# Gate maxima by scan instructions, a split last tile in the first output projection, one slab pool with two early weights, and low halves of the output weights on VectorE, in a two-layer hybrid decoder step

## The chip, the cores and the metric

The kernel runs on one NeuronCore of a Trainium2 chip. The metric is the device time of one execution in microseconds (us). The engines are TensorE (PE in the rows), VectorE (DVE), ScalarE (ACT) and GpSimd (POOL), each with an instruction queue of its own; all DMAs of this kernel are issued on the queue of SyncE (SP).

## The reference, cut to what matters

One step of a two-layer trunk for a prompt of 1024 positions and eight samples of one position each, 1032 columns in all, in float32, with 1024 features.

```python
h = x
# layer 0
u = rmsnorm(h) @ w_in_even            # q|k|v|gate | z|xBC|dt
att = dilated_attention(q, k, v) * silu(gate)
y   = rmsnorm(ssd_scan(conv(xBC), dt) * silu(z))
h   = h + concat(att, y) @ w_out_even # 1536 -> 1024
# layer 1
u = rmsnorm(h) @ w_in_odd             # q|k|v|o|i|f|z
bcum = cumsum(log_sigmoid(f))         # in chunks of 128
m_t  = maximum(bcum + m_prev, running max of (bcum_t - bcum_s + i_s))
m_new = max(b_last + m_prev, max(b_last - bcum + i))   # carried over 8 chunks
h = h + (mlstm(q, k, v, m_t) * silu(z)) @ w_out_odd    # 2048 -> 1024
y = rmsnorm(h)
```

## The kernel before, in words

Activations lie transposed, features on the partitions and columns along the free axis. Every large product is made of three matmuls in a rounded float32 type: each operand is split into a high half (a cast on ScalarE, L91) and a low half (a subtraction, L92, on VectorE or GpSimd), and high x high, high x low and low x high are summed in PSUM. Weights come by DMA as 128x1024 tiles into three raw buffers (L94) and are split by the class `Weights` (L116), whose list `engs` names the engines that take the low halves in turn; `next` keeps one weight ahead.

Slabs (`S`, L57) are [128,1040] tiles of a pool of 15; layer 0 and layer 1 each open such a pool of their own, layer 1 after layer 0 has closed (L1107, L1110). TMP (L78) is a pool of four [128,520] tiles that residuals, squares, gate values and loads share. `eap` (L575) has two [128,512] tiles.

The order in which the work is written down is not the order on the engines: a planner in the build puts instructions of each engine in an order by that writing order and by when it expects operands and buffers to be free. Small closures are put between matmul groups by hand: `bpump` takes from the list `bg`, `dpump` from `dq` (the samples' attention and the samples' state steps), `slot` from `gsteps` (the gates of layer 1).

The stages that the change touches, in order of time:

- Gates z of layer 0 (L990 to L1032): twelve weights f, three column chunks c each. After f < 8 and c == 2 one step of the samples' state (`dss_step`, L825) is taken from `dq`, two at f == 6; a step uses two TMP tiles (`dso`, L831) and GpSimd and VectorE in turn (L835 to L838). Chunks with f >= 8 also load the attention into TMP (`al`, L1006).
- First output projection (`wqo`, L987, all low halves on GpSimd; L1082 to L1102): two column halves hv (512 and 520 columns), eight output tiles f each, `out_f` (L914). In hv = 0 the second half's operand is made beside it by `mix_y(1)` (L867): eight gate products (L884) with `z` loaded into TMP (L874), squares and their sum (L213), then the column norm by matmuls with a vector of ones (`stat_r`, L184), a broadcast (`r_bcast`, L203), and the splits. In hv = 1 the norm of layer 1 for the first half is made (`xn1_piece(0)`, L1048).
- The boundary (L1103, L1104): after the last tile, `xn1_piece(1)` makes norm and operands `yh`, `yl` for the 520 columns of the second half; six of its eight low halves are on GpSimd (L1064). Layer 1 then opens its pools, its first two weights are split (L1504), and for each of three column chunks of 344 two projections run, with the gate projections `pg` (L1151) after chunks 0 and 1 and after chunk 2 (L1506 to L1511).
- Gates of layer 1 (L1183 to L1231): a running maximum over 128 positions in seven doubling steps of two VectorE instructions (L1191, L1192), and a recurrence over eight chunks on one partition, two instructions each (L1199, L1200).
- Second output projection (`wqf`, L1569, low halves on VectorE and GpSimd in turn; L1631 to L1670). Its last tile is already done in two column pieces: `out_f` with `done` (L940) finishes a piece, starts its norm, and puts these steps between the matmuls of the next piece (L946).

Of the kernel before, what the change touches and what calls it, by code (L numbers as in the profile page):

```python
# [21 lines left out]
SLABS0 = 15  # L22
SLABS1 = 15
# [6 lines left out]
def body(ctx, tc, I, O):  # L30
# [15 lines left out]
    dr = pool("dr", 1, space=DRAM)  # L46
    cur = {}

    def scope(tag, slabs):
        st = ctx.enter_context(ExitStack())  # L50
        cur["stack"] = st
        cur["cst"] = pool("cst" + tag, 1, st)
        cur["sm"] = pool("sm" + tag, 2, st)
        cur["slab"] = pool("slab" + tag, slabs, st)
        return st

    def S(name, dt=F32):  # L57
        return cur["slab"].tile([128, 1040], dt, tag="S", name=name)
# [97 lines left out]
    layer0 = scope("0", SLABS0)  # L156
# [565 lines left out]
    def ssd_prep(c, g):  # L722
# [7 lines left out]
        if c > 0:  # L730
            ea = eap.tile([128, 512], F32, tag="ea", name="ea")
# [135 lines left out]
    def mix_y(hv, alloc):  # L867
# [46 lines left out]
    def out_f(wq, nk, ops, hv, res, dst, done=None):  # L914
# [72 lines left out]
    wqo = Weights([(I["wo0"][j], 1024) for _ in range(2) for j in range(12)], (G,))  # L987
    gA = []
    ssd_pump(1)
    for f in range(12):  # L990
# [11 lines left out]
        for c in range(3):  # L1002
# [10 lines left out]
            if f < 8:  # L1013
# [3 lines left out]
                if c == 2:  # L1017
                    dpump(1 + (f == 6))
# [29 lines left out]
    def xn1_piece(hv, src):  # L1048
        n = 520 if hv else 512
        c0 = 512 * hv  # L1050
        box = {}

        def stat():
            box["r"] = stat_r([hacc[:, hv * 520 : hv * 520 + n]], n, 1.0 / 1024, 1.0)
# [4 lines left out]
        def out(k):  # L1059
            if hv == 0:  # L1060
# [3 lines left out]
            sink(src(k)[:, :n], normw[:, 1, k : k + 1], box["p"], hi, lo, G if hv and k % 4 < 3 else V, xsm[:, k] if hv else None)  # L1064

        bg.extend([stat, bcast])
        bg.extend(lambda k=k: out(k) for k in range(8))

    def h1_reload(k):
        t = eap.tile([128, 512], F32, tag="ea", name="h1r")  # L1070
# [7 lines left out]

    h1 = None
    ops = [[operand(hv, u) for u in range(2)] for hv in range(2)]  # L1080
    wst = wstream(wqo)
    for hv in range(2):  # L1082
# [4 lines left out]
        for f in range(8):  # L1087
            dst = pairs(h1)(f, 0, n) if hv else None
            dst = out_f(wst, 12, ops, hv, I["xT"][:, f, c0 : c0 + n], dst)
# [9 lines left out]
            elif f == 1:  # L1099
                xn1_piece(0, h1_reload)  # L1100
# [9 lines left out]
    layer1 = scope("1", SLABS1)  # L1110
    cur["w"] = pool("wp1", 2, layer1)
    wq1 = Weights([(I[n_][h, j], 1024) for h in range(8) for n_, cnt in (("wq", 4), ("wz", 2)) for j in range(cnt)], (V,))
# [27 lines left out]
    mp = C("mp", [1, 9, 8])  # L1140
# [3 lines left out]
    G.memset(mp[:, 0], -1e30)  # L1144
# [30 lines left out]
    def gates_b():  # L1175
        pb_ = X("pbc")
        PE.matmul(pb_[:, 0:64], tri, lff[:, 0:64], start=True, stop=True)
        PE.matmul(pb_[:, 64:128], ones, lff[:, 0:64], start=True, stop=True)
        V.tensor_copy(bcm, pb_[:, 0:64])
        V.tensor_copy(btot, pb_[:, 64:128])  # L1180
        V.tensor_tensor(av, igf[:, 0:64], bcm, sub)

    def gates_c2():  # L1183
# [4 lines left out]
        for j in range(7):  # L1188
            s_ = 1 << j
            a_, b_ = gp[j % 2], gp[(j + 1) % 2]  # L1190
            V.tensor_tensor(b_[:, s_:], a_[:, s_:], a_[:, : 128 - s_], mx)  # L1191
            V.tensor_copy(b_[:, :s_], a_[:, :s_])  # L1192

    def gates_d():
        gmax = gt["gp"][1]
# [5 lines left out]
        store(O["mm"], mp[:, 8])  # L1201

    def gates_e():
        gmax = gt["gp"][1]
        mpf = mp.rearrange("p a b -> p (a b)")
        pm = X("pmb")
        PE.matmul(pm[:, 0:72], ones[0:1, :], mpf, start=True, stop=True)
        PE.matmul(pm[:64, 128:129], mpf[:, 0:64], ones[0:1, 0:1], start=True, stop=True)
# [24 lines left out]
    gsteps = deque([gates_a, rest, rest, gates_b, rest, gates_c2, rest, gates_d, gates_e, rest, gates_f])  # L1233
# [335 lines left out]
    wqf = Weights([(I["wo1"][f][:, o * 1024 : o * 1024 + 1024], 1024) for _ in range(2) for f in range(8) for o in range(2)], (V, G))  # L1569
# [275 lines left out]
```

## Time and profile before

| | us |
|---|---|
| median of 3 runs | 2179.12 |
| lowest and highest run | 2178.77 and 2180.62 |
| the profiled execution's own time | 2182.44 |
| its span, first to last instruction | 2180.5 |
| idle time of TensorE within the span (2180.5 less 2104.4 busy) | 76.1 |

The profiled execution took 3.3 us more than the median. In the rows, PE is TensorE's matmul side and PEld its weight loads; a bracket at the end of a timeline row gives the engine's idle time before it and what ended that. PEclk is the granted share of TensorE's clock: 1.00 is 2.4 GHz and 0.50 is 1.2 GHz.

### The profile page before, as it was taken

How to read it: one execution, taken by the hardware profiler on the slowest of the kernel's cores; microseconds unless marked ns; L12 is line 12 of the kernel's file. 1: busy time of each engine (PE TensorE's matmuls, PEld its weight loads, DVE VectorE, ACT ScalarE, POOL GpSimd, SP SyncE). 2: the span in 40 equal slices, each digit the busy share in tenths (PEclk: the TensorE clock that was granted, in tenths of full speed). 3: DMA queues.
4: the chain of work that ended last, by engine and by line, in shares of the span. 5: the costliest groups of instructions: out<-in, count | busy, mean ns of one | idle time of the engine just before them, and what ended most of it. 6: DMA issues, size and time to landing. Idle time of an engine off the chain costs nothing.

```text
span 2180.5 us, 35187 instructions
## 1 busy us (share of the span) xinstructions
PE 2104.4 (97%) x12913; PEld 1884.0 (86%) x12913; DVE 1356.9 (62%) x3153; ACT 847.8 (39%) x1828; POOL 665.8 (31%) x1089
## 2 busy tenths in 40 slices
PE   7999988999899999999999999999999999999998
PEld 6877777998789798989989889898898998987798
DVE  7444388668887644844548566575565655756754
ACT  5434334455425332533425334253343433434331
POOL 4222143014552343052141321413214223242321
PEclk9999999999999999999999999999999999999999
DMA  4222152134555552311314123132241232406753
GB/s 158 71 74 77 41 158 76 53 99 157 170 188 158 163 187 66 107 45 40 95 38 133 57 89 125 33 115 79 81 131 29 95 100 67 150 24 208 251 172 100
DMA packets 161918, 232.29 MB, mean 107 GB/s; under 512 B 41170, under 2 KB 106690, under 8 KB 161746
## 3 DMA queue, kind: packets, MB, share of 16 engines
q1 hardware_dynamic: 161746, 230.04, 33.5%
q8 instruction: 102, 1.67, 0.3%
q14 instruction: 70, 0.57, 0.1%
HBM read 174.35 MB, written 55.62 MB: 105 GB/s over the span
## 4 chain that ended last, share of the span: by engine, by line
PE 56%; DVE 3%; POOL 2%; DMA 2%; issue 1%; ACT 1%; POOLq 0%; DVEq 0%; SPq 0%; ACTq 0%
PE pf L113 24%; PE pvo L113 16%; PE po L927 8%; PE mN L113 2%; PE mC L113 2%; PE mS L1275 1%; DMA dC<-in_mcs 1%; POOL mCl L92 1%; PE mH L1336 1%; PE mS L1277 1%; DVE dnum L1402 0%; DVE dC L1398 0%; DMA mE<-mud 0%; POOL md L1261 0%; PE prb L203 0%
## 5 line engine op out<-in xcount | busy, mean ns | idle before, releaser
L113 PE MATMUL pf<-yl,wh 128*128 128x344 f32 x1152 | 369.5, 321 | 2.1 <-POOL yl L92 2.1
L113 PE MATMUL pf<-yh,wh 128*128 128x344 f32 x1152 | 371.0, 322 | 0.0
L113 PE MATMUL pf<-yh,wl 128*128 128x344 f32 x1152 | 368.6, 320 | 0.2 <-DVE wl L92 0.2
L91 ACT CAST wh<-raw 128x1024 fp32r<-128x1024 f32 x128 | 133.8, 1046 | 228.8 <-PE pf L113 90.3
L113 PEld LDWEIGHTS pf<-yl,wh 128*128 128x128 f32 x1152 | 217.0, 188 | 3.0 <-POOL yl L92 3.0
L113 PEld LDWEIGHTS pf<-yh,wh 128*128 128x128 f32 x1152 | 216.8, 188 | 1.4 <-ACT craw L238 1.0
L113 PEld LDWEIGHTS pf<-yh,wl 128*128 128x128 f32 x1152 | 216.6, 188 | 0.8 <-DVE wl L92 0.7
L113 PE MATMUL pvo<-wvh,yh 128*128 128x512 f32 x512 | 205.8, 402 | 0.0
L113 PE MATMUL pvo<-wvl,yh 128*128 128x512 f32 x512 | 201.7, 394 | 0.0
L113 PE MATMUL pvo<-wvh,yl 128*128 128x512 f32 x512 | 201.6, 394 | 0.0
L113 PE MATMUL pf<-xh,wh 128*128 128x344 f32 x576 | 195.6, 340 | 2.7 <-ACT gth L232 2.7
L92 DVE TENSOR_TENSOR wl<-raw,wh 128x1024 fp32r<-128x1024 f32 x88 | 111.6, 1268 | 133.7 <-ACT wh L91 133.5
L113 PE MATMUL pf<-xh,wl 128*128 128x344 f32 x576 | 187.5, 326 | 0.0
L113 PE MATMUL pf<-xl,wh 128*128 128x344 f32 x576 | 187.5, 326 | 0.0
L92 POOL TENSOR_TENSOR wl<-raw,wh 128x1024 fp32r<-128x1024 f32 x40 | 99.3, 2483 | 220.0 <-ACT wh L91 220.0
L1263 DVE TENSOR_SCALAR mx<-mx,mbs,md 128x256 f32<-128x256 f32 x64 | 26.5, 413 | 177.3 <-POOL md L1262 177.3
L927 PE MATMUL po<-oh,wl 128*128 128x512 f32 (+2 forms) x384 | 123.9, 323 | 5.2 <-DVE wl L92 4.2
L246 DVE SCALAR_TENSOR_TENSOR cout<-craw,mcw,cout 128x1024 f32<-128x1024 f32 x96 | 123.1, 1283 | 8.3 <-ACT cout L244 6.8
L927 PE MATMUL po<-oh,wh 128*128 128x512 f32 (+2 forms) x384 | 124.1, 324 | 0.9 <-ACT oh L91 0.9
L927 PE MATMUL po<-ol,wh 128*128 128x512 f32 (+2 forms) x384 | 123.7, 322 | 0.0
L113 PEld LDWEIGHTS pf<-xh,wh 128*128 128x128 f32 x576 | 110.7, 192 | 8.8 <-issue 5.1
L113 PEld LDWEIGHTS pvo<-wvh,yl 128*128 128x128 f32 x512 | 96.1, 188 | 22.2
(435 smaller groups left out, 5200.4 us busy)
## 6 DMA issues: line engine op xcount, KB each, us to landing
raw<-in_wo SPq DMA_DIRECT2D x56, 512.0 KB
raw<-in_wq SPq DMA_DIRECT2D x32, 512.0 KB
raw<-in_wvo SPq DMA_DIRECT2D x32, 512.0 KB
dC<-in_mcs SPq DMA_DIRECT2D x32, 512.0 KB
out_mcs<-dC SPq DMA_DIRECT2D x32, 512.0 KB
raw<-in_wf SPq DMA_DIRECT2D x24, 512.0 KB
sE<-acd SPq DMA_DIRECT2D x16, 512.0 KB
raw<-in_wz SPq DMA_DIRECT2D x16, 512.0 KB
```

Source lines behind the costliest of these rows:

```text
L91: A.copy(hi, src)
L92: eng.tensor_tensor(lo, src, hi.bitcast(F32), sub)
L113: PE.matmul(out, l, r, start=i == 0, stop=i == n - 1)
L246: V.scalar_tensor_tensor(o[:, :NP], raw[:, j : j + NP], w4[:, j : j + 1], o[:, :NP], mult, add)
L927: PE.matmul(p[:, :m], wt[:, ws], at, start=i == 0 and q == 0, stop=i == nk - 1 and q == 2)
L1263: V.tensor_scalar(x, x, bs[:, 6:7], d[:, 2:3], sub, mult)
L1275: PE.matmul(pS[:, 0:128], hd["k"][j][:, tok], hd["q"][j][:, tok], start=j == 0, stop=j == 1)
L1277: PE.transpose(pS[:, 128 + j * 128 : 256 + j * 128], hd["k"][j][:, tok], ident)
L1336: PE.transpose(pH[:, j * 128 : j * 128 + 128], x[:, j * 128 : j * 128 + 128], ident)
```

## The change

Six edits. (1) The running maximum over 128 positions and the recurrence over eight chunks become one scan instruction each; the recurrence lies on eight partitions, one per head, and is brought there and back by small matmuls; one more `rest` is put into the list of gate steps. (2) The last tile of the first output projection goes through the two-piece path of `out_f`; each piece's norm follows it, with alternate low halves on GpSimd. (3) One pool of 15 slabs serves both layers. (4) The first two weights of layer 1 are fetched before and during that last tile, into slabs. (5) `z` of the second half loads into `eap` in place of TMP, and the samples' state steps come one position earlier (the last of them at f == 7, c == 0). (6) All low halves of both output projections' weights are on VectorE.

```diff
-    def scope(tag, slabs):
+    slab = pool("slab", SLABS)
+    def scope(tag):
...
-        def __init__(self, srcs, engs=(V,), first=()):
+        def __init__(self, srcs, engs=(V,), first=(), slabs=0):
...
-                th = p.tile([128, 1024], F32R, tag="wh", name="wh")
-                tl = p.tile([128, 1024], F32R, tag="wl", name="wl")
+                if self.slabs:
+                    self.slabs -= 1
+                    th, tl = (S(x, F32R)[:, :1024] for x in ("wh", "wl"))
+                else:
+                    th = p.tile([128, 1024], F32R, tag="wh", name="wh")
+                    tl = p.tile([128, 1024], F32R, tag="wl", name="wl")
...
-            z = TMP("zl") if hv else eap.tile([128, 512], F32, tag="ea", name="zl")
+            z = eap.tile([128, 520], F32, tag="ea", name="zl")
...
-                    if steps and i in (7, 11):
+                    if steps and i in ((7, 11) if nk == 16 else (4, 10)):
...
-    wqo = Weights([...], (G,))
+    wqo = Weights([...])
...
-                if c == 2:
-                    dpump(1 + (f == 6))
+                if c == 2 and f < 7 or f == 0 and c == 1 or f == 7 and c != 1:
+                    dpump(1)
...
-    def xn1_piece(hv, src):
+    def xn1_piece(c0, n, accs, src):
...
-            sink(src(k)[:, :n], normw[:, 1, k : k + 1], box["p"], hi, lo, G if hv and k % 4 < 3 else V, xsm[:, k] if hv else None)
-        bg.extend([stat, bcast])
-        bg.extend(lambda k=k: out(k) for k in range(8))
+            x = src(k)
+            scaled(x, x, normw[:, 1, k : k + 1], box["p"])
+            split(hi, lo, x, G if c0 and k % 2 else V)
+            if c0 == 512 and k == 7:
+                wq1.fetch()
+            if c0 + n == T:
+                split(xsm[:, k, 0:8], xsm[:, k, 8:16], x[:, n - 8 : n])
+        return [stat, bcast] + [lambda k=k: out(k) for k in range(8)]
+
+    def xn1_tail(dst, o, n):
+        store(h1d[7][:, 512 + o : 512 + o + n], dst[:, o : o + n])
+        sq = TMP("sq")[:, :n]
+        A.activation(sq, dst[:, o : o + n], AF.Square)
+        return xn1_piece(512 + o, n, [hacc[:, 520 + o : 520 + o + n], sq], lambda k: pairs(h1)(k, o, n))
...
+    wq1 = Weights([...], (V,), slabs=2)
...
+            if hv and f == 7:
+                bpump(40)
+                wq1.fetch()
+            dst = out_f(wst, 12, ops, hv, I["xT"][:, f, c0 : c0 + n], dst, xn1_tail if hv and f == 7 else None)
...
-    xn1_piece(1, lambda k: pairs(h1)(k, 0, 520))
-    bpump(40)
...
-        for j in range(7):
-            s_ = 1 << j
-            a_, b_ = gp[j % 2], gp[(j + 1) % 2]
-            V.tensor_tensor(b_[:, s_:], a_[:, s_:], a_[:, : 128 - s_], mx)
-            V.tensor_copy(b_[:, :s_], a_[:, :s_])
+        V.tensor_tensor_scan(gp[1], gp[0], gp[0], -1e30, mx, mx)
+        V.tensor_scalar(gr2[:, 0:8], blk[:64, 0:8], gp[1][:, 127:128], None, mult)
...
-        PE.transpose(pgl[:1, 0:64], gmax[:, 127:128], ident[:64, :64])
-        for c in range(8):
-            V.tensor_tensor(mp[:, c + 1], mp[:, c], pgl[:1, c * 8 : c * 8 + 8], mx)
-            V.tensor_tensor(mp[:, c + 1], mp[:, c + 1], btot[0:1, c * 8 : c * 8 + 8], add)
+        PE.matmul(pgl[:8, 0:16], selh, gr2, start=True, stop=True)
+        gl = SM("gl", [8, 16], 1)
+        V.tensor_copy(gl, pgl[:8, 0:16])
+        V.tensor_tensor_scan(mp[:, 1:9], gl[:, 0:8], gl[:, 8:16], -1e30, mx, add)
+        V.tensor_tensor(mp72, ident[:8, :8].unsqueeze(1).broadcast_to([8, 9, 8]), mp.unsqueeze(2).broadcast_to([8, 9, 8]), mult)
...
-    wqf = Weights([...], (V, G))
+    wqf = Weights([...])
```

## Rows read from the trace of the kernel before

**Rows 1.** The page, busy time of each engine in the whole span.

```profile
PE 2104.4 (97%) x12913; PEld 1884.0 (86%) x12913; DVE 1356.9 (62%) x3153; ACT 847.8 (39%) x1828; POOL 665.8 (31%) x1089
```

**Rows 2.** Busy time by stretch: boundary, gates of layer 1, rest of layer 1's heads.

```profile
core 0: us, PE busy (x) PEld busy (x) DVE busy (x) ACT busy (x) POOL busy (x), PEclk, DMA share, GB/s
...
837.60:883.02 45.42, 40.76 (x238) 36.16 (x238) 28.19 (x53) 18.46 (x37) 15.27 (x25) 0.92 0.11 28
883.02:927.54 44.52, 44.52 (x286) 43.52 (x286) 35.27 (x99) 21.01 (x39) 2.54 (x5) 1.00 0.45 122
927.54:1972.00 1044.46, 1037.90 (x6134) 945.26 (x6133) 625.81 (x1585) 399.90 (x827) 316.53 (x672) 1.00 0.26 81
```

**Rows 3.** The boundary: two timeline rows of PE, a wait, a chain row.

```profile
837.32 0.28 PE L927 MATMUL po<-ao,wl 128*128 128x256 f32 x1
839.62 1.18 PE L184 MATMUL pst<-ones,ssdst 128*128 128x1 f32 x10 [2.02 <-DVE ssdst L213]
...
PE pf L113 <- POOL yl L92: 2.1, 3, 0.9
...
869.23 7.55 PE pf L113 x48
```

**Rows 4.** Timeline of PE in the second output projection's split last tile.

```profile
2170.79 0.38 PE L184 MATMUL pst<-ones,sq 128*128 128x1 f32 x2 [0.85 <-ACT sq L1626]
...
2172.97 1.22 PE L203 MATMUL prb<-dg,ones 128*128 128x128 f32 x4 [1.35 <-DVE dg L202]
```

**Rows 5.** Timeline of PE at the norm in `mix_y(1)`.

```profile
725.68 1.99 PE L184 MATMUL pst<-ones,yac 128*128 128x1 f32 x10 [3.13 <-DVE yac L213]
727.60 1.22 PE L927 MATMUL po<-mh,wh 128*128 128x512 f32 x2
...
731.93 0.40 PE L927 MATMUL po<-ml,wh 128*128 128x512 f32 x1
```

**Rows 6.** Gate products of `mix_y`: all (min/median/max ns), two of them, a GpSimd split.

```profile
L884 DVE TENSOR_TENSOR cout<-cout,zl x16: 676/694/2826, 623.6 to 722.3; 128x512 f32<-128x512 f32 x8, 128x520 f32<-128x520 f32 x8
...
703.68 2.83 DVE L884 TENSOR_TENSOR cout<-cout,zl 128x520 f32<-128x520 f32 x1 [0.40 <-DMA zl<-zd]
...
722.32 1.85 DVE L884 TENSOR_TENSOR cout<-cout,zl 128x520 f32<-128x520 f32 x1 [1.28 <-DMA zl<-zd]
...
703.56 2.39 POOL L92 TENSOR_TENSOR wl<-raw,wh 128x1024 fp32r<-128x1024 f32 x1 [5.52 <-ACT wh L91]
```

**Rows 7.** Timeline at the last state step of the samples: ACT, then PE.

```profile
648.96 0.45 ACT L231 COPY gz<-pf 128x344 f32<-128x344 f32 x1 [8.29 <-DVE y_b L838]
...
649.82 0.63 PE L113 MATMUL pf<-xh,wh 128*128 128x344 f32 x1 [2.73 <-ACT gth L232]
...
653.37 0.32 PE L113 MATMUL pf<-xh,wh 128*128 128x344 f32 x1
```

**Rows 8.** Low halves of weights on the page; PE's wait for GpSimd from 1965 on.

```profile
L92 DVE TENSOR_TENSOR wl<-raw,wh 128x1024 fp32r<-128x1024 f32 x88 | 111.6, 1268 | 133.7 <-ACT wh L91 133.5
L92 POOL TENSOR_TENSOR wl<-raw,wh 128x1024 fp32r<-128x1024 f32 x40 | 99.3, 2483 | 220.0 <-ACT wh L91 220.0
...
PE po L927 <- POOL wl L92: 1.0, 2, 0.6
```

**Rows 9.** A low half late on VectorE in the second output projection: DVE, then PE.

```profile
2040.22 0.88 DVE L1398 SCALAR_TENSOR_TENSOR dC<-dvb,dkw,dC 128x256 f32<-128x256 f32 x2 [4.62 <-ACT dC L1394]
...
2046.16 1.22 DVE L92 TENSOR_TENSOR wl<-raw,wh 128x1024 fp32r<-128x1024 f32 x1
...
2047.43 0.79 PE L927 MATMUL po<-oh,wl 128*128 128x512 f32 x1 [4.18 <-DVE wl L92]
```

**Rows 10.** The doubling steps of the running maximum, line L1191.

```profile
L1191 DVE TENSOR_TENSOR gp<-gp x7: 205/267/284, 903.6 to 911.3; 64x127 f32<-64x127 f32 x1, 64x126 f32<-64x126 f32 x1, 64x124 f32<-64x124 f32 x1, 64x120 f32<-64x120 f32 x1
```

**Rows 11.** VectorE's waits from 688 to 770 (total, times, longest).

```profile
DVE cout L884 <- DMA zl<-zd: 8.9, 5, 4.9
DVE ao L92 <- ACT ao L91: 6.0, 2, 4.6
```

More of the change, by code (lines that the diff above doesn't have):

```diff
@@ L21 @@
 KB = 3
-SLABS0 = 15
-SLABS1 = 15
+SLABS = 15
 PS_MM = 3
@@ L53, in scope @@
         cur["sm"] = pool("sm" + tag, 2, st)
-        cur["slab"] = pool("slab" + tag, slabs, st)
         return st
     def S(name, dt=F32):
-        return cur["slab"].tile([128, 1040], dt, tag="S", name=name)
+        return slab.tile([128, 1040], dt, tag="S", name=name)
     def XS(name, dt=F32R):
@@ L116, in body @@
     class Weights:
-        def __init__(self, srcs, engs=(V,), first=()):
+        def __init__(self, srcs, engs=(V,), first=(), slabs=0):
+            self.slabs = slabs
             self.engs = deque(engs)
@@ L153, in proj_c @@
         return p
-    layer0 = scope("0", SLABS0)
+    layer0 = scope("0")
     xs0 = []
@@ L730, in ssd_prep @@
         if c > 0:
-            ea = eap.tile([128, 512], F32, tag="ea", name="ea")
+            ea = eap.tile([128, 520], F32, tag="ea", name="ea")[:, :512]
             for u in range(2):
@@ L985, in ssd_pump @@
             ssd_b()
-    wqo = Weights([(I["wo0"][j], 1024) for _ in range(2) for j in range(12)], (G,))
+    wqo = Weights([(I["wo0"][j], 1024) for _ in range(2) for j in range(12)])
     gA = []
@@ L1063, in out @@
             hi, lo = (t[k][:, c0 : c0 + n] for t in (xh1, xl1))
-            sink(src(k)[:, :n], normw[:, 1, k : k + 1], box["p"], hi, lo, G if hv and k % 4 < 3 else V, xsm[:, k] if hv else None)
-        bg.extend([stat, bcast])
-        bg.extend(lambda k=k: out(k) for k in range(8))
+            x = src(k)
[11 more added lines that the diff above has]
+        return xn1_piece(512 + o, n, [hacc[:, 520 + o : 520 + o + n], sq], lambda k: pairs(h1)(k, o, n))
     def h1_reload(k):
-        t = eap.tile([128, 512], F32, tag="ea", name="h1r")
+        t = eap.tile([128, 520], F32, tag="ea", name="h1r")[:, :512]
         load(t, h1d[k][:, 0:512])
@@ L1077, in attB @@
         return r
+    wq1 = Weights([(I[n_][h, j], 1024) for h in range(8) for n_, cnt in (("wq", 4), ("wz", 2)) for j in range(cnt)], (V,), slabs=2)
     h1 = None
@@ L1088, in body @@
             dst = pairs(h1)(f, 0, n) if hv else None
-            dst = out_f(wst, 12, ops, hv, I["xT"][:, f, c0 : c0 + n], dst)
+            if hv and f == 7:
+                bpump(40)
+                wq1.fetch()
+            dst = out_f(wst, 12, ops, hv, I["xT"][:, f, c0 : c0 + n], dst, xn1_tail if hv and f == 7 else None)
+            if hv and f == 7:
+                continue
             store(h1d[f][:, c0 : c0 + n], dst)
@@ L1107, in body @@
     layer0.close()
-    layer1 = scope("1", SLABS1)
+    layer1 = scope("1")
     cur["w"] = pool("wp1", 2, layer1)
-    wq1 = Weights([(I[n_][h, j], 1024) for h in range(8) for n_, cnt in (("wq", 4), ("wz", 2)) for j in range(cnt)], (V,))
     gb = C("gb", [128, 16], I["gb"].partition_broadcast(128))
@@ L1139, in body @@
     nm2 = C("nm2", [128, 64])
-    mp = C("mp", [1, 9, 8])
+    mp = C("mp", [8, 9])
+    mp72 = C("mp72", [8, 9, 8])
+    gr2 = C("gr2", [64, 16])
+    selh = C("selh", [64, 8])
+    V.reduce_sum(selh, ident[:64, :64].rearrange("p (c h) -> p h c", h=8), AX.X)
     mud = D("mud", [2, 64, 128])
@@ L1143, in body @@
     G.memset(lf, 0.0)
-    G.memset(mp[:, 0], -1e30)
+    G.memset(mp[:, 0:1], -1e30)
     g32 = S("g32")
@@ L1178, in gates_b @@
         PE.matmul(pb_[:, 64:128], ones, lff[:, 0:64], start=True, stop=True)
+        PE.matmul(pb_[:64, 128:129], lff[:, 0:64], ones[:, 0:1], start=True, stop=True)
         V.tensor_copy(bcm, pb_[:, 0:64])
+        V.tensor_tensor(av, igf[:, 0:64], bcm, sub)
         V.tensor_copy(btot, pb_[:, 64:128])
-        V.tensor_tensor(av, igf[:, 0:64], bcm, sub)
+        V.tensor_scalar(gr2[:, 8:16], blk[:64, 0:8], pb_[:64, 128:129], None, mult)
     def gates_c2():
@@ L1231, in gates_f @@
         V.tensor_scalar(nm2, nm2, 2.0, None, mult)
-    gsteps = deque([gates_a, rest, rest, gates_b, rest, gates_c2, rest, gates_d, gates_e, rest, gates_f])
+    gsteps = deque([gates_a, rest, rest, gates_b, rest, gates_c2, rest, gates_d, rest, gates_e, rest, gates_f])
     dcq = deque()
@@ L1567, in body @@
             tail.append(lambda g=g: dml_group(g))
-    wqf = Weights([(I["wo1"][f][:, o * 1024 : o * 1024 + 1024], 1024) for _ in range(2) for f in range(8) for o in range(2)], (V, G))
+    wqf = Weights([(I["wo1"][f][:, o * 1024 : o * 1024 + 1024], 1024) for _ in range(2) for f in range(8) for o in range(2)])
     hld = deque()
```

17 lines of the change are left out of this document (7 added, 10 removed).

## The prediction

> **What bounds the kernel now.** I read the page's busy times first: TensorE is busy for 2104.4 of 2180.5 us [rows 1]. So an edit gains only where it closes one of TensorE's gaps or shortens its work, and all gaps together are 76.1 us. The table of busy time by stretch then says where gaps are not: while the gates of layer 1 are computed TensorE is busy for 44.52 of 44.52 us, and in the rest of layer 1's heads it idles for 6.6 us in 1044 [rows 2]. It also says where one is: the boundary between the layers has 40.76 us busy in 45.42, at a mean granted clock of 0.92 [rows 2]. Last I read TensorE's waits and the timelines around them. Three stops lie on the change's path: the boundary [rows 3], the norm in `mix_y(1)` [rows 5] and the last state step of the samples [rows 7].
>
> **The boundary** (edits 2, 3, 4). The stretch is 45.42 us long. Its work at full clock: 144 projection matmuls at 7.55/48 = 0.157 us, 22.7 [rows 3]; 48 gate matmuls of the same 344 columns, priced alike, 7.6; ten norm sums, 1.2 [rows 3]; ten broadcast matmuls, by the four in 1.22 us at the lower clock 3.0, at the higher half of that, 1.5 [rows 4]. That makes 33.0, so 12.4 us are lost: 2.0 before the sums [rows 3], 2.1 on GpSimd's low halves [rows 3], and the rest to the lower clock and small waits. After the change the last evacuation, square and sum handle 256 columns, not 520, and the addition L213 drops out of the chain. The same code already runs at the end of the second projection, where the wait before the sums is 0.85 us, not 2.0 [rows 4]. Its next wait, 1.35 us before the broadcast [rows 4], I cost at nothing: two projections over columns that are already normed, with weights now split, stand ready to cover it (2 x 24 x 0.157 = 7.5 us); without that cover it costs 1.35. Two sum lists where there was one add ten small matmuls, 1.2 us by the ten of [rows 3], half of them beside the second piece; I charge 1.0. The second weight pair is fetched only after the first piece's eight outputs: twelve VectorE instructions (eight scalings, four low halves) of half the width of a gate product's 0.69, 4.2 us [rows 6]. The wait for it is at least 0 (other chunks run first) and at most those 4.2 with a cast and a low half behind them, both priced at 1.27 [rows 8], less the first weight's 24 matmuls: 4.2 + 2.5 - 3.8 = 2.9. I take 1.0, nearer the low end, since the first piece's columns give TensorE other work. Left over: 0.85 + 1.0 + 1.0 = 2.9; gain 9.5. Its ends: 10.5, if the pair is on time, and 3.7, if the wait before the sums stays at 2.0, the pair costs 2.9 and the clock falls again for 2.8 as in the next part (12.4 - 2.0 - 1.0 - 2.9 - 2.8).
>
> **The norm in `mix_y(1)`** (edits 5, 6). TensorE waits 3.13 us for the last square sum [rows 5]. Then it runs at the lower clock: the ten sums take 1.99 for 1.18 [rows 3, 5], and the ten matmuls from 727.60 to 731.93 take 4.33, at the later 0.232 us each 2.3 (512 columns by 0.157 x 512/344). Together 3.1 + 0.8 + 2.0 = 5.9 us. What makes the sum late? A gate product takes 0.69 us in the median, but 2.83 at 703.68, under a GpSimd split that runs from 703.56 to 705.95, and 1.85 at 722.32, after 1.28 of waiting for `z` [rows 6]. So the low halves on GpSimd cost VectorE 2.14 and 1.16 us in these two places, for 1.27 that VectorE needs to do one itself [rows 8]. On the two together the edit saves 3.30 - 2.54 = 0.8 us, and the wait for `z`, whose buffer no longer competes with residuals and squares, up to 1.28 at the last product and 8.9 over the stage [rows 6, 11]. 0.8 + 1.28 = 2.1 falls short of 3.13; a few more us of the 8.9 make up the rest. I count the full 5.9; the ends are 5.9 and 0.
>
> The Trainium skill, page "SBUF — State Buffer", section "Who interferes with whom", says that a VectorE instruction with two SBUF inputs and a GpSimd instruction that reads SBUF take turns at a shared port, and the loser stands still for the other's whole duration. The row at 703.68 agrees: 2.39 of GpSimd's split, and the product ends 0.56 after it. By this rule alone each split could cost VectorE 2.4, so that the edit would save 1.1 each time, 2.3 in the two places where the rows show 0.8, and the sum would keep its 5.9 with more to spare.
>
> **The last state step** (edit 5). At 648.96 ScalarE had idled 8.29 us for VectorE's reduction of that step to give a TMP buffer back; TensorE then waited 2.73 us for PSUM, and ran twelve matmuls in 3.55 us that take 1.9 at the full clock [rows 7]: 4.4 us. In the new order this step comes two chunks earlier, ahead of the chunks that also hold `al` in TMP, so two more TMP tiles are free. I count 4.4; the ends are 4.4 and -2 (the step stops an earlier chunk for nearly as long as now). The step's DMAs move along with it, past two stores of `z` on SyncE's queue; the step before it no longer comes as one of a pair, so its load has as long as now.
>
> **Low halves on VectorE** (edit 6). All 40 of GpSimd's full-width low halves belong to the two projections, so VectorE, 62% busy over the span [rows 1], gets 40 x 1.27 = 51 us more work; TensorE has waited 1.0 us for GpSimd's in the second one [rows 8]. Gain 1.0. The new wait: a low half that GpSimd did while VectorE stood still now stands still with it. One such stop is in the trace: VectorE idles 4.62 us for a state tile, the low half follows six us later, TensorE waits 4.18 [rows 9] and, as in the norm's case, loses some 2 more to the lower clock: 6.2. The ends for this edit are +6.2 (that stop goes, as VectorE is no longer held up by GpSimd) and -12.4 (two more). I take -2.2, a third of one stop, because a weight is kept one ahead.
>
> **Scans** (edit 1). Seven steps at 0.27 us and their copies, and the sixteen recurrence steps, give way to two scans, which no row shows: between 0.28, one pass like the longest step, and 1.9, all seven [rows 10]. Either way 0: TensorE has no idle time in this stretch [rows 2]. If that cover were gone, one gate chain of some microseconds would show. The two small matmuls that are added stand on TensorE's path, 0.2 us at the price of a norm sum. The further `rest` moves the last gate steps by one chunk, with the heads' first use later still: 0. One pool of slabs by itself: 0, it only lets the two early weights in.
>
> **Sum.** 9.5 + 5.9 + 4.4 + 1.0 - 2.2 - 0.2 = 18.4 us. The profiled execution took 2182.44, 3.3 above the median of 2179.12; it gives 2164.0 on its own time, and on the median 2160.7, which I round to 2161. All three stops closed and nothing new: 2179 - 21 - 1 (pair on time) - up to 6.2 = 2151 at best.
>
> **Rivals.** *Part of it.* The boundary closes and only one of the other stops does, or neither: for it speaks that the rows account for 2.1 of the 3.13 us only, and that the state step may find the same buffers taken earlier. Time: 2161 + 4.4 to 2161 + 10.3, so 2165 to 2172.
>
> *Early weights that are not early.* The change would not do what it says if slabs are short: eight hold the second half's operand and four `h1`, so the first pair fits in 15 and the second must wait for an operand slab, which the last tile frees. Should the pair come late, the boundary gains 3.7; if the other two stops stay and half a new one (3.1, priced in the slower case) comes with VectorE's added work, the time is 2179.1 - 3.7 - 1.0 + 3.1 = 2177.5. Against it: the operand is read for the last time eight weight columns into the second piece, before the boundary.
>
> *Slower.* VectorE's order becomes the bound of the output projections: low halves are queued behind products and splits that wait for loads. Such waits in the trace: 4.9 for `z`, 4.6 for the attention operand [rows 11], 4.62 for a state tile [rows 9]. Each can become a stop of 6.2. If VectorE's added work also keeps the norm in `mix_y(1)` late (no 5.9), what is gained is 9.5 + 4.4 + 1.0 = 14.9; three stops give 2179.1 - 14.9 + 18.6 = 2182.8, four 2189.0, and from four on it is slower by over 0.2%. Against it: GpSimd's part vanishes from VectorE's stretched instructions, and a weight ahead covers some 5.6 us (24 matmuls of 512 columns).
>
> The Trainium skill, page "TensorE: Matmul & The Clock Gate", section "Architectural detail: the array is 16× 32×32, not 1× 128×128", says that ScalarE and VectorE take their instructions strictly first in, first out. By that rule this rival works as told; the low half in [rows 9], which runs right in the middle of VectorE's queue while TensorE waits, agrees.
>
> **How the numbers follow.** The forecast, all three stops closed or nearly: 0.48, 2153 to 2165. Better than that, since the low-half stop goes too: 0.07. Part of it: 0.27, 2165 to 2172. Early weights not early: 0.11, 2175 to 2181. Slower: 0.07, about 2189. Within 0.2% means 4.4 us, about what a measurement of this kernel can tell from no change, so faster is below 2174.7: 0.48 + 0.07 + 0.27 = 0.82; same 0.11; slower 0.07. The range for 8 in 10 leaves out the slower case and most of the third rival: 2152 to 2174.
>
> **What would show it.** Right: at the end of the first projection PE's wait before the sums is near 0.9 us and the next projection follows at clock 1.00; no wait of 3 us for `yac`, no ACT wait of 8 us for `y_b`; the stretch from the last output matmul to the first gate transpose is 35 to 37 us, not 45.42. Wrong: new PE waits on DVE `wl` of 2 us and more in either projection, a PE wait for the second weight pair, or gate products that still wait for `z`.

## The result, and the profile after

The changed kernel takes **2161.6 us** in the median of five runs (2158.0 to 2169.9), the kernel before 2180.6 (2178.8 to 2182.6) on the same chip: a ratio of 0.991, 95% interval 0.989 to 0.993. The forecast was 2161, in a range of 2152 to 2174. A repetition of the changed kernel on another chip gave 0.992 (0.991 to 0.994). So the total is right. Whether its terms are is another matter: two of them were wrong, by 4.4 and 7.5 us in opposite directions.

The profiled execution of the changed kernel took 2158.71 us, with a span of 2156.9, against 2180.5 before. First the page's busy time of each engine, as in [rows 1]:

```profile
PE 2097.2 (97%) x12926; PEld 1880.9 (87%) x12926; DVE 1350.3 (63%) x3176; ACT 849.6 (39%) x1837; POOL 561.9 (26%) x1052
```

GpSimd has lost 104 us of work. VectorE, which took it over, is busy for 6.6 us less than before. TensorE's busy time fell by 7 us and its gaps from 76.1 to 59.7.

Next the span cut at four places that both kernels have: the first output matmul of the first projection, the end of its last one, the first gate transpose and the first matmul of the second projection. This is the changed kernel's busy time by stretch (from and to, length, busy time of PE, PEld, DVE, ACT and POOL, then the granted clock and two figures of the DMAs):

```profile
0.00:686.34 686.34, 645.09 (x4151) 559.20 (x4152) 462.71 (x1107) 297.03 (x791) 220.61 (x326) 0.99 0.37 114
686.34:829.08 142.74, 142.40 (x921) 128.85 (x919) 86.59 (x136) 51.55 (x69) 5.57 (x7) 1.00 0.54 174
829.08:865.90 36.82, 35.98 (x232) 32.99 (x230) 25.57 (x55) 17.12 (x43) 9.68 (x24) 1.00 0.18 48
865.90:1955.25 1089.35, 1083.48 (x6425) 990.05 (x6424) 657.21 (x1660) 421.51 (x865) 316.20 (x676) 1.00 0.27 82
1955.25:2156.90 201.65, 190.26 (x1208) 169.81 (x1207) 118.20 (x222) 62.39 (x71) 9.84 (x19) 0.98 0.57 191
```

And the same view of the kernel before, for the stretches that [rows 2] doesn't have:

```profile
0.00:688.92 688.92, 643.59 (x4152) 557.97 (x4152) 464.19 (x1104) 297.29 (x790) 221.86 (x327) 0.99 0.36 112
688.92:837.60 148.68, 144.07 (x902) 129.22 (x900) 78.29 (x109) 48.96 (x66) 57.99 (x26) 0.98 0.55 174
1972.54:2180.50 207.96, 193.37 (x1208) 171.73 (x1207) 124.64 (x207) 62.23 (x71) 51.61 (x34) 0.96 0.56 186
```

[rows 2] cuts the boundary at 883.02; the first gate transpose itself starts at 882.95, so by these four places the boundary was 45.35 us long before, and layer 1's heads 1089.6. The profiled gain of 23.6 us then comes from four places: 2.6 ahead of the first projection, 5.9 inside it, 8.5 at the boundary, and 6.3 in the second projection. Layer 1's heads between them gave 0.2.

| stretch | predicted gain | profiled gain | what the other runs show |
|---|---|---|---|
| start to first projection | 4.4 | 2.6 | none; see below |
| first projection | 5.9 | 5.9 | 5.7 to 6.0 with all edits there, against this profile of before |
| boundary | 9.5 | 8.5 | 36.7 to 36.9 us in every profile with both edits |
| layer 1's heads | -0.2 | 0.2 | 1088.3 to 1090.4 us long in all, with scans or without |
| second projection to the end | -1.2 | 6.3 | 5.1 to 6.7 wherever VectorE makes all low halves |

TensorE's timeline at the three places that the prediction named, in the changed kernel (start, length, engine, line, what; in brackets the idle time before it and what ended it):

```profile
660.29 1.05 PE L188 MATMUL pst<-ones,yac 128*128 128x1 f32 x8 [2.05 <-DVE yac L217]
...
719.78 1.07 PE L188 MATMUL pst<-ones,yac 128*128 128x1 f32 x10
...
829.06 0.41 PE L112 MATMUL pf<-yh,wh 128*128 128x344 f32 x1
...
830.75 0.28 PE L188 MATMUL pst<-ones,sq 128*128 128x1 f32 x2
...
833.68 0.71 PE L207 MATMUL prb<-dg,ones 128*128 128x128 f32 x4 [0.84 <-DVE dg L206]
```

The norm in `mix_y(1)` (719.78) no longer waits; [rows 5] had 3.13 there. At the boundary the projection of layer 1 has begun at 829.06, before the sums at 830.75, which therefore wait for nothing, where [rows 3] had 2.02. One wait is left, 0.84 us before the broadcast, and the granted clock is 1.00 instead of 0.92. But at 660.29 there is a stop that the kernel before did not have: the norm of the first half's gate products.

### The profile page after: what moved, and what is told of

The parts are those of the page before. It is cut to its first block, busy times and chain, and to the rows that moved or that the text cites. A ratio compares the mean times of both kernels' runs of the same rounds, so it can differ in the third digit from the quotient of the medians.

```text
span 2156.9 us, 35181 instructions
## 1 busy us (share of the span) xinstructions
PE 2097.2 (97%) x12926; PEld 1880.9 (87%) x12926; DVE 1350.3 (63%) x3176; ACT 849.6 (39%) x1837; POOL 561.9 (26%) x1052
## 3 DMA queue, kind: packets, MB, share of 16 engines
q8 instruction: 102, 1.67, 0.3%
## 4 chain that ended last, share of the span: by engine, by line
PE 78%; DVE 7%; DMA 3%; POOL 3%; issue 2%; ACT 2%; POOLq 0%; SPq 0%; DVEq 0%; ACTq 0%
PE pf L112 32%; PE pvo L112 16%; PE po L931 14%; PE pq L112 4%; PE mN L112 2%; PE mC L112 2%; PE pS L428 1%; PE pO L487 1%; PE mS L1294 1%; PE pT L470 1%; DMA sE<-acd 1%; POOL mCl L91 1%; DVE P L468 1%; PE mH L1355 1%; PE mS L1296 1%
## 5 line engine op out<-in xcount | busy, mean ns | idle before, releaser
L91 DVE TENSOR_TENSOR wl<-raw,wh 128x1024 fp32r<-128x1024 f32 x128 | 161.7, 1263 | 156.3 <-ACT wh L90 155.7
L250 DVE SCALAR_TENSOR_TENSOR cout<-craw,mcw,cout 128x1024 f32<-128x1024 f32 x96 | 123.1, 1284 | 13.4 <-ACT cout L248 11.9
L112 PEld LDWEIGHTS pf<-xl,wh 128*128 128x128 f32 x576 | 110.7, 192 | 4.3 <-issue 4.3
```

The source lines that it names most:

```text
L91: eng.tensor_tensor(lo, src, hi.bitcast(F32), sub)
L112: PE.matmul(out, l, r, start=i == 0, stop=i == n - 1)
L250: V.scalar_tensor_tensor(o[:, :NP], raw[:, j : j + NP], w4[:, j : j + 1], o[:, :NP], mult, add)
```

## Experiments

**The changed kernel once more.** The edit is an empty line.

> The changed kernel with nothing altered but a blank line. Its five runs lay between 2158.0 and 2169.9 us, a spread of 12 where the kernel before had 4. Theory A: the spread belongs to the kernel (some stop comes and goes with the arrival of transfers): again between 2157 and 2170, and a profile with another time shows which stop. Theory B: it was that one chip's: the runs lie within 5 us of each other, near 2160.

Median 2164.5, five runs from 2163.0 to 2167.3, ratio 0.9924 (0.9911 to 0.9938). The runs lie within 5 us, as theory B has it, but around another value than on the first chip; the two sets together are ten runs from 2158 to 2170 with a median of 2163.8. The profile (2164.49) tells where the two profiled executions differ: 691.6 us to the first projection instead of 686.3, and by at most 0.4 us in any other stretch. Among the profiles that share all code of that first stretch with the changed kernel it took 686.3, 688.1, 691.6, 691.8, 693.3 and 693.9. The repetition's row of that stretch:

```profile
0.00:691.61 691.61, 649.50 (x4152) 563.60 (x4153) 464.31 (x1108) 297.93 (x791) 221.52 (x326) 0.98 0.36 113
```

TensorE does the same matmuls in both, and of the 5.3 us between them 4.4 are busy time (649.5 for 645.1), at a granted clock of 0.98 in the mean for 0.99; its gaps differ by only 0.9. The offset builds up in steps: 1.5 us at the `pO` matmuls near 290, 3.4 by 508, 4.8 by 551. Single waits that both profiles have differ (before `pcb` on ScalarE 1.67 us in one, 2.80 in the other). What makes them vary was not found. For the reading of everything below it means: a stretch behind 690 us can be compared to some tenths of a microsecond, the total only to some 3 us.

**The second projection's low halves.** GpSimd makes every other one again.

```diff
-    wqf = Weights([...])
+    wqf = Weights([...], (V, G))
```

> The low halves of the second output projection's weights alternate between VectorE and GpSimd again, as before the change; all else as changed. If that move closed the stop of 4.18 us for a weight's low half and the lower clock after it: 6 us slower, near 2167, and the stop or its like is in the profile. If that stop was a matter of one run: within 2 us of the changed kernel, and no wait of over 2 us for a low half.

Median 2169.6, 5.1 above the repetition of the changed kernel in the same set; ratio 0.9946 (0.9933 to 0.996). The stretch of the second projection takes 207.3 us instead of 202. The stop is back, within 0.3 us of both waits in [rows 9]. First VectorE, then TensorE of this kernel, then all steps on `dnum` of the samples' state (min/median/max in ns):

```profile
2029.95 0.88 DVE L1417 SCALAR_TENSOR_TENSOR dC<-dvb,dkw,dC 128x256 f32<-128x256 f32 x2 [4.32 <-ACT dC L1413]
...
2037.17 0.51 PE L931 MATMUL po<-oh,wl 128*128 128x512 f32 x1 [3.90 <-DVE wl L91]
...
L1421 DVE SCALAR_TENSOR_TENSOR dnum<-dC,dq,dnum x124: 471/480/2604, 1149.7 to 2043.6; 128x256 f32<-128x256 f32 x124
```

**The same edit alone.** The kernel before, with all low halves of the second projection on VectorE and nothing else.

```diff
-    wqf = Weights([...], (V, G))
+    wqf = Weights([...])
```

> The kernel before with one edit alone: the second output projection's low halves all on VectorE. If this edit by itself takes away the stop of 4.18 us and the lower clock behind it: that projection (first output matmul to the end) 202 to 203 us for 208.0, and 5 to 6 us faster than before, near 2175. If it needs the other edits: 207 to 208 us, and no gain.

Median 2175.2 of 11 runs, 6.0 below the kernel before; ratio 0.9976 (0.9967 to 0.9984). The stretch takes 201.4 us, 6.6 less than before. By itself, then, this edit gives the whole gain of the second projection's stretch. The wait of 4.18 us in [rows 9] is 1.02 here. The reason is in the same kind of row, from 1975 to 2100 us, this time of the kernel with the one edit:

```profile
L1402 DVE SCALAR_TENSOR_TENSOR dnum<-dC,dq,dnum x31: 476/480/483, 2003.3 to 2049.7; 128x256 f32<-128x256 f32 x31
```

and of the kernel before, over the same window:

```profile
L1402 DVE SCALAR_TENSOR_TENSOR dnum<-dC,dq,dnum x31: 469/476/2621, 2004.3 to 2053.9; 128x256 f32<-128x256 f32 x31
```

One step of 0.48 us takes up to 2.62 us while GpSimd splits a weight, and never more than 0.48 when it doesn't. In the kernel before, ScalarE waits 7.4 us for `dC` to be loaded and VectorE 5.7 us behind it in this window; with the one edit they wait 4.1 and 3.8. So VectorE's idle 4.62 us in [rows 9], which the prediction took as a given, was made in part by the low halves on GpSimd. On SyncE's queue the load of the next state tiles stands right behind the store of one that VectorE has just finished. The store, the loads and ScalarE's wait for the first of them, in the kernel before and then in the kernel with the one edit:

```profile
2031.89 0.34 SPq L1403 DMA_DIRECT2D out_mcs<-dC  x1
2032.32 2.12 SPq L1345 DMA_DIRECT2D dC<-in_mcs  x3
2039.03 2.44 ACT L1394 ACTIVATE dC<-dC,dss 128x1024 f32<-128x1024 f32 x2 [4.98 <-DMA dC<-in_mcs]
...
2030.36 0.34 SPq L1403 DMA_DIRECT2D out_mcs<-dC  x1
2030.79 1.93 SPq L1345 DMA_DIRECT2D dC<-in_mcs  x3
2035.91 1.15 ACT L1394 ACTIVATE dC<-dC,dss 128x1024 f32<-128x1024 f32 x1 [2.78 <-DMA dC<-in_mcs]
```

Counted from the projection's first matmul (1972.54 and 1973.05), the loads are issued 59.8 us into it before and 57.7 with the edit, and the first of them is used after 66.5 and 62.9. So 2.0 of the 3.6 us are a late issue behind a late store. Three VectorE instructions ahead of that store are drawn out, each beside a split on GpSimd:

```profile
1998.64 2.19 DVE L1374 TENSOR_TENSOR dss<-dvb 128x1 f32<-128x1 f32 x1 [0.48 <-ACT dvb L1370]
2010.85 2.50 DVE L213 TENSOR_TENSOR yacc<-yacc,sq 128x512 f32<-128x512 f32 x1 [0.73 <-ACT sq L211]
2021.73 2.45 DVE L1402 SCALAR_TENSOR_TENSOR dnum<-dC,dq,dnum 128x256 f32<-128x256 f32 x1
```

With the one edit the same three take 0.16, 0.69 and 0.48 us. In the other 1.6 us the load itself took longer, 6.7 us for 5.1 from issue to use; why is not shown. The low half of [rows 9] is 3.6 us later too (73.6 and 70.0 us into the projection).

The Trainium skill, page "SBUF — State Buffer", section "Who interferes with whom", says that a VectorE instruction with two inputs in SBUF contends with a GpSimd instruction that reads SBUF. The rows agree: 2621 ns at most with GpSimd's splits, 483 without.

**The first projection's low halves, and the buffer of `z`.** Three kernels: the first edit undone, the second undone, and both.

```diff
-    wqo = Weights([...])
+    wqo = Weights([...], (G,))
```

> The low halves of the first output projection's weights are GpSimd's again (40 splits of 2.4 us beside VectorE's gate products); the buffer of z stays as changed. Theory P (the splits held VectorE's gate products up, and that made the norm late): the wait before the norm's square sums comes back, 4 to 6 us slower, near 2166, with gate products of 2 us and more. Theory Q (the wait for z's buffer did it): 0 to 1 us.

```diff
-            z = eap.tile([128, 520], F32, tag="ea", name="zl")
+            z = TMP("zl") if hv else eap.tile([128, 520], F32, tag="ea", name="zl")
```

> z of the second half is loaded into the pool of temporaries again, which residuals and squares share; the low halves stay on VectorE. Theory P (GpSimd's splits made the norm late): 0 to 1 us. Theory Q (the wait for z's buffer did): VectorE waits for z by up to 8.9 us over the stage, the wait before the norm's sums comes back, 4 to 6 us slower, near 2166.

> Both edits for the first projection are undone together: GpSimd makes its low halves and z of the second half sits in the pool of temporaries. Alone, the first lengthened the first projection (first to last output matmul) from 142.8 to 145.2 us and the second not at all, where the kernel before had 148.7. Theory R (the two together made the stop): the projection takes 147 to 149 us, the whole about 2168 to 2170, and the wait before the norm's sums is 2 us or more again. Theory S (the rest of the 5.9 us came from another edit, the order of the state steps or the places of the background steps): 145 us again, about 2166.

(The 40 splits named in the first expectation are those of both projections; the first has 24.)

| undone | first projection, us | its norm's wait, us | median, us | ratio, 95% interval |
|---|---|---|---|---|
| nothing | 142.74 | 0 | 2164.5 | 0.9924 (0.9911 to 0.9938) |
| low halves | 145.22 | 0 | 2167.2 | 0.9934 (0.9921 to 0.9946) |
| `z` buffer | 142.97 | 0 | 2163.7 | 0.9916 (0.9902 to 0.9929) |
| both | 152.19 | 2.79 | 2173.0 | 0.9955 (0.9937 to 0.9973) |

Neither theory P nor theory Q holds. The wait before the norm's sums comes back only when both edits are undone (theory R), and then the stretch is even 3.5 us longer than in the kernel before, 1.3 of which are a wait of TensorE for one of GpSimd's low halves and 0.7 one for a square sum; TensorE's busy time is 2.1 us longer (146.15 for 144.07, with 921 matmuls for 902, as the split tile's first norm now lies in this stretch), and its other waits are 0.5 shorter. The kernel with both undone, TensorE and then the gate products from 690 to 740 us:

```profile
730.90 1.99 PE L188 MATMUL pst<-ones,yac 128*128 128x1 f32 x10 [2.79 <-DVE yac L217]
...
L888 DVE TENSOR_TENSOR cout<-cout,zl x8: 684/700/1758, 703.8 to 727.6; 128x520 f32<-128x520 f32 x8
```

The last product starts at 727.6 of this profile, 34.6 us into the stretch; in the changed kernel at 697.3, after 11.0, with `z` back in the temporaries at 720.6, after 35.6, and with the low halves back at 704.1, after 11.9. With one edit in place the products are either early, or late but not drawn out (their maximum is 701 ns with only `z` back), and either is enough. What the low halves alone cost, 2.5 us, is at other waits inside the stretch: 1.5 instead of 0.3 us before broadcasts, 0.7 before a square sum, and 0.6 more busy time of TensorE.

**The order of the samples' state steps.** The old order, with the last two steps as a pair.

```diff
-                if c == 2 and f < 7 or f == 0 and c == 1 or f == 7 and c != 1:
-                    dpump(1)
+                if c == 2:
+                    dpump(1 + (f == 6))
```

> The samples' state steps stand in the old order, the last two as a pair; all else as changed. Theory T (the prediction's: closing the last step's stop gains 4.4 us): about 2166, with the 8 us wait of ScalarE and the 2.7 us wait of TensorE back. Theory U (the stop goes, but the norm of the first half's gates, a wait of 2.0 us and the lower clock behind it, takes its place, so the order is worth nothing): within 1.5 us of the changed kernel, and that norm's wait under 1 us here.

Median 2163.8, ratio 0.991 (0.9897 to 0.9924): no loss. The waits of TensorE from 600 to 692 us (in total, times, longest), in this kernel:

```profile
PE pf L112 <- ACT gth L236: 2.9, 1, 2.9
PE pst L188 <- DVE yac L217: 0.7, 1, 0.7
PE prb L207 <- DVE dg L206: 0.5, 1, 0.5
```

and in the repetition of the changed kernel:

```profile
PE pst L189 <- DVE yac L218: 2.0, 1, 2.0
PE pf L113 <- ACT gth L237: 1.4, 1, 1.4
PE pxt L753 <- DVE sx L760: 1.0, 1, 1.0
```

The stop for PSUM is back, as both theories have it, and the norm's is smaller, as theory U has it. Laid side by side, the old order starts this part 1.0 us ahead, is 3.6 behind after its stop at 652, and level again (0.0) at 665.5, where the other one waits for its norm; at the end of the part, at 680, it is 0.1 us ahead. Closing one stop opened the other.

All profiles bear this out, with less scatter than the whole first stretch has. Take the last 18 chunks of 24 matmuls ahead of the first projection. In the changed kernel the first nine of them run from the first of these rows to the second, and in the kernel before from the third to the 649.82 of [rows 7], which is the stop:

```profile
604.18 0.32 PE L112 MATMUL pf<-xh,wh 128*128 128x344 f32 x1
644.83 0.32 PE L112 MATMUL pf<-xh,wh 128*128 128x344 f32 x1
...
606.03 0.32 PE L113 MATMUL pf<-xh,wh 128*128 128x344 f32 x1
```

These nine take 43.75 to 43.91 us in all four profiles of the old order (the kernel before, the one with one edit alone, this one, and the last one below) and 40.65 to 40.83 in the other ten. So closing the stop is worth 3.1 us in each of them. The nine chunks behind them take 38.7 to 39.6 with the old order, and 41.4 to 44.1 in the six profiles that share all code of this part with the changed kernel. Together that is 82.6 to 83.6 against 82.0 to 84.8: what was gained is given back.

**The norm later.** Two empty steps ahead of the first half's norm, once with the new order of the state steps, once with the old.

```diff
-        bg.extend([rest, rest, stat, rest, bcast])
+        bg.extend([rest] * (2 if hv else 4) + [stat, rest, bcast])
```

> The changed kernel with two more empty background steps ahead of the first half's norm, so that TensorE asks for its square sums one chunk (3.8 us) later. If the norm's stop is what took the place of the state step's (a wait of 2.0 us and the lower clock behind it): that wait goes, 3 to 4 us faster, near 2159, faster than both kernels. If the stop only moves on to the outputs of that norm or to the first output matmul: within 1 us of the changed kernel.

> The same two empty steps, and the samples' state steps in the old order. If the new order is worth something once the norm's stop is away (theory U): 3 to 5 us slower than with the new order and the two steps, near 2163, with TensorE's wait of 2.9 us for PSUM back. If the order is worth nothing at all: the same as with the new order, near 2159.

Both expectations fail. With the new order the median is 2169.1 (ratio 0.9949, 0.9934 to 0.9963), slower; with the old order 2162.3 (0.992, 0.9904 to 0.9936), the same as the changed kernel. In the first of the two the sums at 665.56 wait for nothing, but the broadcast behind them does, twice. TensorE, then VectorE:

```profile
673.00 0.68 PE L207 MATMUL prb<-dg,ones 128*128 128x128 f32 x4 [2.63 <-DVE dg L206]
676.42 1.22 PE L207 MATMUL prb<-dg,ones 128*128 128x128 f32 x4 [2.42 <-DVE dg L206]
...
672.14 0.52 DVE L1031 SCALAR_TENSOR_TENSOR gA<-gz,al 128x344 f32<-128x344 f32 x1 [1.12 <-DMA al<-ad]
672.58 0.48 DVE L206 TENSOR_SCALAR dg<-ident,str 128x128 f32<-128x128 f32 x2
675.46 0.70 DVE L888 TENSOR_TENSOR cout<-cout,zl 128x520 f32<-128x520 f32 x1 [2.41 <-DMA zl<-zd]
676.08 0.48 DVE L206 TENSOR_SCALAR dg<-ident,str 128x128 f32<-128x128 f32 x2
```

VectorE's two short `dg` instructions stand behind one that waits for `al`, a product of the attention gates, and one that waits for `z`, a gate product of the second half; with `z` in `eap` these reach this far forward. So the mechanism of the prediction's slower rival, a short VectorE instruction on TensorE's path that is queued behind products waiting for loads, is real, in a place that the prediction did not look at. With the norm later, the old order is even 6.9 us faster than the new one, so the new one is worth nothing either way. No version was found that beats the changed kernel by more than its spread.

**The boundary without early weights, and with the last tile whole.**

```diff
-    wq1 = Weights([...], (V,), slabs=2)
...
-            if c0 == 512 and k == 7:
-                wq1.fetch()
...
                 bpump(40)
-                wq1.fetch()
...
     cur["w"] = pool("wp1", 2, layer1)
+    wq1 = Weights([...], (V,))
```

> The first two weights of the second layer are fetched after the boundary's norm, as before the change; the last tile stays split and the slabs stay one pool. The boundary (last output matmul to first gate transpose) took 45.4 us before and 36.8 changed. If the early weights carry the gain: 41 to 44 us, with TensorE waiting for a weight after the first piece is normed, 4 to 7 us slower in all, about 2167. If the split does: 37 to 38 us, about 2162.

```diff
-            dst = out_f(wst, 12, ops, hv, I["xT"][:, f, c0 : c0 + n], dst, xn1_tail if hv and f == 7 else None)
-            if hv and f == 7:
-                continue
+            dst = out_f(wst, 12, ops, hv, I["xT"][:, f, c0 : c0 + n], dst)
...
+    bg.extend(xn1_piece(512, 520, [hacc[:, 520:1040]], lambda k: pairs(h1)(k, 0, 520)))
+    bpump(40)
```

> The last tile of the first projection is one piece of 520 columns in its norm again; the early weights stay. If the split carries the gain: 41 to 45 us in the boundary, with the wait of 2.0 us before the sums back, 4 to 8 us slower, about 2167. If the early weights do: 37 to 39 us, about 2163. If each alone is worth little and only both together close the gap: both this kernel and the one without early weights stand above 41 us.

Without the early weights the median is 2177.9 of 12 runs (ratio 0.9983, 0.9972 to 0.9993): nearly all of the change's gain is lost. The boundary takes 51.5 us, longer than the 45.4 of the kernel before. Its stretch, then TensorE, then VectorE:

```profile
830.85:882.38 51.53, 39.43 (x231) 36.20 (x230) 25.15 (x56) 19.84 (x45) 11.89 (x26) 0.87 0.09 22
...
847.22 0.65 PE L112 MATMUL pf<-yh,wl 128*128 128x344 f32 x1 [9.32 <-DVE wl L91]
...
845.95 2.35 DVE L91 TENSOR_TENSOR wl<-raw,wh 128x1024 fp32r<-128x1024 f32 x2
```

ScalarE cast both weights by 834.7, but VectorE makes their low halves at 845.95, behind all low halves that it makes of the two pieces (eight of sixteen; GpSimd makes the others). In the kernel before they ran at 840.99 and 843.50, ahead of them. The split gives TensorE an earlier start and VectorE more low halves to put in front of the weights: eight of half width, where it had two of full width. The early fetch is what puts the weights in front: in the changed kernel one low half runs at 823.90 and the other at 845.58, and TensorE waits for neither. The Trainium skill, page "TensorE: Matmul & The Clock Gate", section "Architectural detail: the array is 16× 32×32, not 1× 128×128", says that VectorE takes its instructions strictly in order; the row agrees, with an input ready 11 us before the instruction that uses it.

With the last tile whole the median is 2163.3 (ratio 0.9916, 0.9903 to 0.993), within the spread of the changed kernel. The stretches show what the total can't:

```profile
691.77:832.87 141.10, 140.76 (x903) 127.24 (x903) 84.69 (x131) 50.19 (x67) 4.33 (x5) 1.00 0.54 174
832.87:874.60 41.73, 38.37 (x237) 33.30 (x236) 28.52 (x55) 16.45 (x35) 10.61 (x21) 1.00 0.17 45
```

The first projection and the boundary together take 182.8 us, against 179.6 in the changed kernel (142.74 + 36.82), because the norm of the first piece has moved from the one to the other: the split is worth 3.3 us. The early weights, by the same sum, are worth 14.7 (142.73 + 51.53 = 194.3). For a common base take 142.74 + 45.35 = 188.1, the boundary of before behind a projection without its norm's stop; this base is put together from two kernels, and no run has it. Early weights alone gain 5.3 on it, the split alone loses 6.2, and the two together gain 8.5. The expectation that the two might only work together is half right. With the tile whole the sums wait for nothing either, so the early weights alone close the 2.0 us of [rows 3]; TensorE's wait for GpSimd's low halves, 2.1 us in [rows 3], is still 1.8 there although GpSimd makes only every other one, so it is the split that closes that.

**The gate scans.** The seven steps and the recurrence again, without the further empty step.

> The gate maxima by seven steps and sixteen recurrence steps again, without the extra empty step; all else as changed. As predicted, the scans are worth nothing, since TensorE has no idle time there: within 1.5 us of the changed kernel, and first gate transpose to the second projection's first matmul 1089 to 1090 us. Rival: the chain is on the path of the first head, 2 us or more slower, and that stretch is longer by as much.

```diff
-        V.tensor_tensor_scan(gp[1], gp[0], gp[0], -1e30, mx, mx)
+        for j in range(7):
+            s_ = 1 << j
+            a_, b_ = gp[j % 2], gp[(j + 1) % 2]
+            V.tensor_tensor(b_[:, s_:], a_[:, s_:], a_[:, : 128 - s_], mx)
+            V.tensor_copy(b_[:, :s_], a_[:, :s_])
...
```

Median 2161.1 of six runs (2156.7 to 2168.0), ratio 0.9919 (0.9902 to 0.9936): no difference. The 40 us behind the first gate transpose are filled with TensorE's work in both kernels; in this one:

```profile
873.48:913.48 40.00, 40.00 (x259) 39.27 (x259) 31.76 (x93) 19.76 (x35) 2.37 (x5) 1.00 0.49 104
```

The changed kernel's row for its own 40 us has 40.00 (x260) too, with 30.19 of VectorE instead of 31.76. The stretch of layer 1's heads takes 1088.3 us here; two profiles with the scans have 1088.5 and 1088.6, so nothing can be read from the one microsecond to the 1089.4 of the changed kernel.

## Why the prediction was right, step by step

**The boundary, 9.5 predicted, 8.5 measured.** The mechanism is the predicted one, and two sizes were off. What was to be left over, 0.85 before the sums and 1.0 for the second weight pair, is nothing: the matmuls of the next projection cover the sums, and the second low half is in time. The broadcast's wait, costed at nothing, is 0.84. In return TensorE's own work is 35.98 us and not the 33.0 and 1.0 of the sum. What the prediction lacks is that the split is harmful without the early weights: the rival "early weights that are not early" was priced at a gain of 3.7 at the boundary, and the kernel without them loses 6.2 there. So what this rival says of a late weight pair holds, and its price was 9.9 us too kind, though that kernel leaves the early fetch out and was not short of slabs. The rival's total of 2177.5 next to the measured 2177.9 is a coincidence, as it put in a new stop of 3.1 and the loss of two other gains.

**The norm in `mix_y(1)`, 5.9 predicted, 5.9 measured.** The step that accounted for it, 0.8 and 1.28 us of 3.13 and "a few more" of the 8.9 that VectorE waits for `z`, added what does not add. Either edit alone closes the stop; only without both does it stand.

**The last state step, 4.4 predicted, none measured.** This is the step that failed. The stop of [rows 7] did shrink, as told: the 2.73 us for PSUM became 0.8 in two waits, or 1.4 in the repetition, and the nine chunks up to it got 3.1 us shorter. But the prediction did not ask what is late next: the norm of the first half's gate products, some 10 us later, takes 2.0 us, with the lower clock behind it, and the nine chunks behind it lose that again. The profiled 2.6 us are not evidence of a gain: this stretch took 688.9 and 689.9 us in the two profiles of the old order without the other edits, 691.6 in the old order with them, and 686.3 to 693.9 in six of the new one, 690.8 in the mean.

**Low halves on VectorE, a loss of 1.2 predicted, a gain of 6.3 measured** in the second projection. Both values stood in the text. The end "+6.2, that stop goes, as VectorE is no longer held up by GpSimd" is what happened (with the 1.0 counted beside it 7.2, to the measured 6.3), and I took "a third of one stop" in its place, because the wait of VectorE for a state tile looked like a matter of its load alone. (A third of 6.2 is 2.1, so the term is also 0.1 off.) It was in part a load issued late (2.0 of 3.6 us), behind VectorE instructions that GpSimd had drawn out, one of 0.48 us fivefold. One wait of 1.6 us for a low half is left in the changed kernel. The slower rival rested on the same misreading: waits of VectorE for loads would remain and gain company, when a third to nearly a half of that waiting (5.7 to 3.8, 7.4 to 4.1) went with the work that the change removed.

**Scans and the further empty step: 0 predicted, 0 measured.** The long scan takes 416 ns, within the bounds of 0.28 and 1.9; the short one, 157, lies below them.

The two misses, 4.4 us too much and 7.5 us too little, came out as a total that is 0.6 us from the median of the first five runs and 2.8 from that of all ten. As a gain, 18.4 us were forecast, and 19.0 and 16.3 measured against the kernel before in the same two sets. That it comes this close is luck: the misses cancel in part, and the first stretch alone varies by more than what is left. Of the forecast's "all three stops closed or nearly", two closed, the third was replaced by another, and a fourth, which the forecast left open, closed too.

## What to carry to other kernels

When work is moved off GpSimd, look at the longest, not the median, of the VectorE instructions beside it, and follow each drawn-out one to the store, the load and the wait behind it: undoing it gained 6 us here, where the longest instruction itself lost 2. When a stop is to be closed, read TensorE's next dependence on the same engine within the following chunks before counting the gain. Two edits at one stop can each be enough, or one of them harmful without the other, so their gains are only known from runs with each undone alone and both together.

## What was not expected of the hardware

- A VectorE step of 0.48 us took 2.60 and 2.62 us under a split on GpSimd; the splits themselves took 5.16 and 5.15 us, for a median of 2.4. Both sides lost.
- The same program took from 686 to 694 us to the same point of its work in six profiles, with no edit in that part, while the first projection and the boundary repeat within 0.3 us wherever their edits are in place.
- A scan over 64 partitions and 128 elements costs 416 ns, a copy of the same tile 282.
